# Multiplying the modulation tiles of a hybrid diffusion layer in runs of two and of four

## The chip, the core and the metric

The kernel runs on one core of a Trainium2 chip. The metric is the device time of one execution in microseconds, as the median of three runs. TensorE is called PE below, VectorE DVE, ScalarE ACT, GpSimd POOL and SyncE SP.

## What is computed

One layer of a diffusion trunk is applied, with the same weights, to 128 context tokens and 128 latent tokens. Cut to what matters here:

```python
mod  = silu(cond) @ w_mod + b_mod      # cond: (2048,), w_mod: (2048, 12288); one cond per token set
sh1, sc1, g1, sh2, sc2, g2 = split(mod, 6)
xm   = rmsnorm(x) * (1 + sc1) + sh1
u, q, k, v, g_s, g_a = split(xm @ w_in)
S    = glu(s5_scan(u))                 # 64 groups, 64 complex states, both directions
A    = windowed_attention(q, k, v)
x   += g1 * ((sigmoid(g_s) * (S @ w_ssm_o) + sigmoid(g_a) * (A @ w_attn_o)) @ w_out)
xm2  = rmsnorm(x) * (1 + sc2) + sh2
x   += g2 * (silu(a) * b @ w_down)     # a, b = split(conv3(xm2 @ w_up)), w_up: (2048, 11264)
```

Everything is float32. The big products are made of three matmuls each: a weight tile is split into a high and a low part (`hi`, `lo`), and so are the activations.

## The kernel before

**Weight tiles.** All weights come from DRAM in tiles of 128 x 1024 floats (512 KB), which SP's queue loads into five buffers (`raw`, `RAW = 5`). A tile of a big product is split by ACT (`hi`, L185) and DVE (`lo`, L186) into one of three pairs of buffers (`HL = 3`), and its raw buffer is free after the split. PE then multiplies it: a tile of `w_up` or `w_in` takes 24 matmuls on the full 128 x 128 array (L396 to L398).

**Modulation tiles.** `mod` has only two columns of activations, one for each token set. A tile of `w_mod` holds four K slices of 256 columns, and `mod_steps` multiplies it straight from its raw buffer, without a split, with four matmuls at L264. They use the array in tiles of 128 x 32, one K slice in each of the four groups of 32 columns. A raw buffer with a modulation tile becomes free when its matmuls are done. The float32 matmuls of L264 stand in the trace as two records each, so eight records are one tile.

**Stages and order.** Steps stand in one list, and `drive()` issues loads and splits ahead of them. First come the modulation tiles and the projections that the scan needs. In the scan stage the steps of the scan are woven with the rest of `w_in`, with `w_attn_o`, and with 96 modulation tiles (gate 1, shift 2, scale 2), each of which is a step of its own. Then come the GLU, the output projections, `w_out`, the second norm, and the up projection. The last 32 modulation tiles (`g2s`, gate 2) belong to the up projection: eight of them (`G2A`, `G2B`) wait in other buffers for the end of `w_out`; the others follow in the same raw buffers as `w_up`, `G2C` of them after every second step of `prep` (the second norm's transposes, L869, and the making of `xm2`), and the rest woven into the first 80% of the first third of the up projection.

The code is recorded in this order, and a scheduler then sets each engine's final order, so the engines' orders differ from the list.

Of the kernel before, what the change touches and what calls it, by code (L numbers as in the profile page):

```python
# [86 lines left out]
RAW, HL, W4, NS4, W2, LOADS = 5, 3, 18, 5, 3, 5  # L87
# [3 lines left out]
NGA2, NGS, SF0, ATT1 = 3, 4, 0.6, 1.0  # L91
ATTP, ATTH, OLS = 1, 300, False
FF0, FF1, MF0, MF1 = 0.0, 1.0, 0.0, 1.0
G2A, G2B, G2S, G2C, LAG2, HP2 = 8, 8, 3, 2, 2, 1000
FIRST_BANKS = ("acc", "acc", "acc", "y")


# [1 line left out]
def tile_hybrid_step(ctx, tc, a):  # L99
# [29 lines left out]
    def PS(shape, tag, bufs=1):  # L129
        return ps.tile(shape, F32, tag=tag, name=tag, bufs=bufs)  # L130

    def f32(x):
        return x.bitcast(F32)
# [6 lines left out]
    def drive():  # L140
        ch = [s for s in steps if s.src is not None]
        raws, hls = {}, {}
        cnt = {"raw": 0, "w4": 0, "first": 0, "s4": 0}
        cap = {"raw": RAW, "w4": LOADS, "first": 8, "s4": G2S}
        state = dict(nr=0, nh=0)

        def issue():
            c = ch[state["nr"]]
            if c.pre is not None:
                c.pre()  # L150
            if c.pool == "raw":
                r = rawp.tile([128, 2, 512], F32, tag="raw", name="raw")
            else:
                r = (T4 if c.pool == "first" else S4)([128, 2, 512], "rw4")
            for o, i in c.src(r):
                nc.sync.dma_start(o, i)
            raws[state["nr"]] = r
            cnt[c.pool] += 1
            state["nr"] += 1

        def ahead():
            while state["nr"] < len(ch) and cnt[ch[state["nr"]].pool] < cap[ch[state["nr"]].pool]:
                issue()

        ahead()
        idx = 0
        for st in steps:
            if st.src is None:
                st.fn()
                continue  # L170
            while state["nh"] < len(ch) and state["nh"] <= idx + HL - 1:
                n = state["nh"]
                while state["nr"] <= n:
                    issue()
                if ch[n].split:
                    if ch[n].hl:
                        th, tl = (ch[n].hl(x).rearrange("p (a b) c -> p a (b c)", a=2) for x in ("hi", "lo"))
                    else:
                        th = hlp.tile([128, 2, 512], F32R, tag="hi", name="hi")
                        tl = hlp.tile([128, 2, 512], F32R, tag="lo", name="lo")  # L180
                    w = slice(0, ch[n].nk)
                    with tc.high_priority(HP), ExitStack() as es:
                        for i in ch[n].after() if ch[n].after else ():
                            es.enter_context(tc.issue_after(i.ins))
                        ACT(th[:, w], raws[n][:, w], AF.Copy)  # L185
                        TT(tl[:, w], raws[n][:, w], f32(th[:, w]), OP.subtract)  # L186
                    hls[n] = (th, tl)
                    cnt[ch[n].pool] -= 1
                state["nh"] += 1
            ahead()  # L190
            if st.split:
                st.fn(*hls.pop(idx))
            else:
                st.fn(raws[idx])
                cnt[st.pool] -= st.frees
            raws.pop(idx)
            idx += 1
# [64 lines left out]
    def mod_mm(acc, kt, rhs, b, start, stop):  # L262
        j = kt % 4
        return MM(acc[32 * j:32 * j + 32], cst[:, kt, 6 - 2 * b:38 - 2 * b], rhs, start=start, stop=stop, skip_group_check=True,  # L264
           tile_position=(0, 32 * j))

    def mod_pp(acc, nb, blocks):
        m = T2([128, 512], "macc")[:, 0:acc.shape[1]]
        nc.vector.transpose(out=m, in_=acc)
        p = acc[:, 0:acc.shape[1] // 64 * nb].rearrange("p (c b s) -> p c b s", b=nb, s=2)  # L270
        mv = m.rearrange("p (c b r) -> p b c r", b=4, r=32)
        for b in range(4):
            MM(p[32 * b:32 * b + 32], i32r, mv[:, b, :, 0:2 * nb], start=True, stop=True, skip_group_check=True, tile_position=(0, 32 * b))
        for b0, c0, nc_, b, n in blocks:
            ks = slice(b0, b0 + nc_ * n)
            v = lambda t: t[:, ks].rearrange("p (b c) -> p c b", b=n)
            TT(modp[:, ks, :].rearrange("p (b c) s -> p c b s", b=n), p[:, c0:c0 + nc_, b:b + n, :],
               v(bT).unsqueeze(3).to_broadcast([128, nc_, n, 2]), OP.add)
# [15 lines left out]
        for s in range(2):  # L294
            nc.sync.dma_start(out[:, s, :], d[s:s + 1, 512 * cg:512 * cg + 512].to_broadcast([128, 512]))

    def mod_steps(gs, pool="raw"):
        nb = len(gs)
        st = {}

        def chunk(b, h, kq):
            def f(raw):
                if (b, h, kq) == (0, 0, 0):
                    st["a"] = PS([128, 512], "mod")
                r = raw.rearrange("p a c -> p (a c)").rearrange("p (k c) -> p k c", k=4)
                prev = None
                for j in range(4):
                    with tc.issue_after(prev.ins) if prev is not None else nullcontext():
                        prev = mod_mm(st["a"][:, 256 * h:256 * h + 256], 4 * kq + j, r[:, j, :], b, b == 0 and h == 0 and kq == 0, b + 1 == nb and kq == 3)
                if b + 1 == nb and (h, kq) == (1, 3):  # L310
                    one = all(g == gs[0] + i for i, g in enumerate(gs))
                    mod_pp(st["a"], nb, [(4 * gs[0], 0, 4, 0, nb)] if one else [(4 * g, 0, 4, i, 1) for i, g in enumerate(gs)])
            return f

        def src(g, h, kq):
            return lambda raw: [(raw, a["w_mod"][MOD_AT[g], h, kq])]
        return [Step(chunk(b, h, kq), src(g, h, kq), False, pool) for b, g in enumerate(gs) for h in range(2) for kq in range(4)]

    def mod_first(k0, n):
        v = a["w_mod_first"]  # L320
# [214 lines left out]
    def mod_phase(p):  # L535
        k0, n = sum(PHASES[:p]), PHASES[p]
        if n < 4:
            return mod_first(k0, n)
        return mod_steps([4 + k0 // 4, k0 // 4], "w4")
# [142 lines left out]
    def weave(main, *fills):  # L682
        n = len(main)
        pos = [0] * len(fills)
        for i, s_ in enumerate(main):
            steps.append(s_)
            for k, fl in enumerate(fills):
                fl, lo, hi = fl if isinstance(fl, tuple) else (fl, 0.0, 1.0)
                while pos[k] < len(fl) and pos[k] * (hi - lo) * n < (i + 1 - lo * n) * len(fl):
                    end = burst(fl, pos[k])  # L690
                    steps.extend(fl[pos[k]:end])
                    pos[k] = end
        for k, fl in enumerate(fills):
            steps.extend((fl[0] if isinstance(fl, tuple) else fl)[pos[k]:])
# [32 lines left out]
    fill += [u for i in range(NGS) for u in gs(i)]  # L727
    modfill = []
    for i in range(8, 20, 4):
        modfill += mod_steps(list(range(i, i + 4)))  # L730
    weave(ssm.stages(), (fill, FF0, FF1), (modfill, MF0, MF1))
    for i in range(NGS, 4):
        steps.extend(gs(i))
# [243 lines left out]
            gfb.append(t)  # L977

    CUT = [0, 8, 15, 22]
    g2s = mod_steps([20, 21, 22, 23])  # L980
    for x in g2s[:G2B]:
        x.pool = "first"

# [18 lines left out]
    g2s = g2s[G2A:]  # L1002
    for p in range(3):
# [3 lines left out]
        if p == 0:  # L1007
# [10 lines left out]
            for k in range(8):  # L1018
                step(lambda k=k: prep(k))
                if k >= LAG2:  # L1020
                    steps.append(ups[k - LAG2])
                    if k % 2 == 0:
                        steps.extend(g2s[:G2C])
                        g2s = g2s[G2C:]
# [11 lines left out]
    def final(s):  # L1036
        row_norm(s, 1)
        for h in range(2):
            t = x1t[2 * s + h]
            row_scale(t, t, s)  # L1040
            nc.sync.dma_start(yout[s][:, 1024 * h:1024 * h + 1024], t)

    drive()


# [459 lines left out]
```

## Time and profile before

| | |
|---|---|
| Time, median of 3 runs | 1558.11 us (1556.1 to 1558.49) |
| Time of the profiled execution | 1556.7 us |
| Its span, first to last instruction | 1554.9 us |
| PE busy | 1507.4 us (97%) |
| DVE, ACT busy | 1005.6 us, 767.1 us |
| Chain that ended last | PE 83%, DMA 6%, DVE 5%, ACT 3% |
| Loads from DRAM | 343.76 MB, 223 GB/s over the span |

The span is what the views of the trace show; the profiled execution's own time is 1.8 us longer. PE is named in most of the chain, so what PE does and what it waits for sets the time; the other engines count where PE waits for them. Overlapping matmuls are counted once in the busy time.

The stages in the trace, in us from its start: modulation and first projections to 260, scan stage 260 to 603, GLU and output projections to 761, second norm and up projection (first third) 761 to 945, the rest of the feed-forward part to 1555.

### The profile page before, as it was taken

The numbers are of one execution on the slowest core, as the hardware profiler recorded it, in microseconds if no ns is written. First come the engines' busy times: TensorE is split into PE (matmuls) and PEld (weight loads), VectorE is DVE, ScalarE is ACT, GpSimd is POOL, SyncE is SP. The second block draws the span as 40 slices with busy tenths as digits, with TensorE's granted clock in tenths as the row PEclk, the third lists the DMA queues.
The fourth block names the chain that finished last, engine by engine and source line by source line (L and its number), as shares of the span: only waits on it lengthen the run. The fifth ranks groups of instructions, "written<-read, shape, count | busy, mean of one in ns | idle before, by whom it ended". The sixth has DMA issues, their size and how long they took to land.

```text
span 1554.9 us, 30702 instructions
## 1 busy us (share of the span) xinstructions
PE 1507.4 (97%) x12575; PEld 1330.7 (86%) x12575; DVE 1005.6 (65%) x1541; ACT 767.1 (49%) x1191; POOL 85.7 (6%) x179
## 2 busy tenths in 40 slices
PE   6999999999899999999899999999999999999997
PEld 5768799788688888988699899889999988999986
DVE  4998687468776666665655556655656655666665
ACT  6334548545555567444544445433544533545543
POOL 2000014022322000000000000000000000000000
PEclk9999999999899999999999999999999999999999
DMA  9999754774577777866556665765555565565563
GB/s 348 362 367 306 267 192 167 249 284 146 181 266 248 264 264 272 312 218 200 190 186 237 222 226 189 246 200 189 170 197 180 177 202 190 176 203 195 172 204 121
DMA packets 104252, 349.28 MB, mean 225 GB/s; under 512 B 13900, under 2 KB 16628, under 8 KB 104112
## 3 DMA queue, kind: packets, MB, share of 16 engines
q1 hardware_dynamic: 98576, 344.20, 64.2%
q0 software_dynamic: 5312, 3.05, 0.9%
q8 instruction: 99, 1.62, 0.4%
q14 instruction: 41, 0.34, 0.1%
q10 hardware_dynamic: 224, 0.08, 0.0%
HBM read 343.76 MB, written 2.46 MB: 223 GB/s over the span
## 4 chain that ended last, share of the span: by engine, by line
PE 83%; DMA 6%; DVE 5%; ACT 3%; issue 1%; POOL 1%; SPq 0%; DVEq 0%; ACTq 0%
PE acc L396 16%; PE acc L397 15%; PE acc L398 15%; PE acc L422 8%; PE acc L423 8%; PE acc L424 8%; PE mod L264 5%; DMA raw<-in_w_in_dram 3%; DMA raw<-in_w_mod_dram 2%; DVE lo L186 2%; PE bu L1376 1%; ACT hi L185 1%; DMA U<-u 1%; ACT CL L1330 1%; POOL U L1317 1%
## 5 line engine op out<-in xcount | busy, mean ns | idle before, releaser
L186 DVE TENSOR_TENSOR lo<-raw,hi 128x1024 fp32r<-128x1024 f32 (+1 forms) x456 | 538.2, 1185 | 448.6 <-ACT hi L185 445.3
L185 ACT ACTIVATE hi<-raw 128x1024 fp32r<-128x1024 f32 (+1 forms) x456 | 468.1, 1028 | 597.2 <-PE acc L398 274.8
L396 PE MATMUL acc<-yh,lo 128*128 128x256 f32 x1408 | 401.3, 285 | 0.5 <-DVE lo L186 0.5
L397 PE MATMUL acc<-yl,hi 128*128 128x256 f32 x1408 | 399.5, 284 | 0.0
L398 PE MATMUL acc<-yh,hi 128*128 128x256 f32 x1408 | 399.3, 284 | 0.0
L396 PEld LDWEIGHTS acc<-yh,lo 128*128 128x128 f32 x1408 | 270.4, 192 | 9.0 <-DVE lo L186 3.0
L397 PEld LDWEIGHTS acc<-yl,hi 128*128 128x128 f32 x1408 | 270.9, 192 | 0.9 <-DVE m L875 0.8
L398 PEld LDWEIGHTS acc<-yh,hi 128*128 128x128 f32 x1408 | 270.8, 192 | 0.0
L396 PE MATMUL acc<-xh,lo 128*128 128x256 f32 x568 | 168.1, 296 | 4.7 <-ACT sig L673 2.6
L398 PE MATMUL acc<-xh,hi 128*128 128x256 f32 x568 | 161.7, 285 | 0.0
L397 PE MATMUL acc<-xl,hi 128*128 128x256 f32 x568 | 161.5, 284 | 0.0
L423 PE MATMUL acc<-lo,ff 128*128 128x512 f32 x352 | 136.9, 389 | 0.0
L424 PE MATMUL acc<-hi,ff 128*128 128x512 f32 x352 | 136.8, 389 | 0.0
L422 PE MATMUL acc<-hi,ff 128*128 128x512 f32 x352 | 127.8, 390 | 0.0
L396 PEld LDWEIGHTS acc<-xh,lo 128*128 128x128 f32 x568 | 108.2, 190 | 22.4 <-issue 8.4
L397 PEld LDWEIGHTS acc<-xl,hi 128*128 128x128 f32 x568 | 108.4, 191 | 1.4 <-issue 0.9
L398 PEld LDWEIGHTS acc<-xh,hi 128*128 128x128 f32 x568 | 108.2, 191 | 0.3 <-issue 0.2
L264 PE MATMUL mod<-raw,cst 128*32 128x256 f32 x960 | 82.6, 404 | 5.6 <-DMA raw<-in_w_mod_dram 4.8
L422 PEld LDWEIGHTS acc<-hi,ff 128*128 128x128 f32 x352 | 66.1, 188 | 14.6 <-issue 1.1
L424 PEld LDWEIGHTS acc<-hi,ff 128*128 128x128 f32 x352 | 66.1, 188 | 13.8
L423 PEld LDWEIGHTS acc<-lo,ff 128*128 128x128 f32 x352 | 66.1, 188 | 13.6
L1317 POOL DMA_DIRECT2D U<-u x128 | 62.6, 497 | 161.7 <-PE bu L1376 138.6
(365 smaller groups left out, 2172.7 us busy)
## 6 DMA issues: line engine op xcount, KB each, us to landing
raw<-in_w_up_dram SPq DMA_DIRECT2D x176, 512.0 KB, 4.2
raw<-in_w_mod_dram SPq DMA_DIRECT2D x120, 512.0 KB, 4.6
raw<-in_w_in_dram SPq DMA_DIRECT2D x88, 512.0 KB, 5.0
raw<-in_w_down_dram SPq DMA_DIRECT2D x88, 512.0 KB, 4.0
rw<-in_w_mod_dram SPq DMA_DIRECT2D x56, 512.0 KB, 5.8
raw<-in_w_out_dram SPq DMA_DIRECT2D x32, 512.0 KB, 4.3
rw<-in_w_mod_first_dram SPq DMA_DIRECT2D x16, 512.0 KB, 7.2
raw<-in_w_in_dram SPq DMA_DIRECT2D x32, 256.0 KB, 5.8
```

The source lines that it names most:

```text
L185: ACT(th[:, w], raws[n][:, w], AF.Copy)
L186: TT(tl[:, w], raws[n][:, w], f32(th[:, w]), OP.subtract)
L264: return MM(acc[32 * j:32 * j + 32], cst[:, kt, 6 - 2 * b:38 - 2 * b], rhs, start=start, stop=stop, skip_group_check=True, tile_position=( ...
L396: MM(o, wl, xh, start=start, stop=False, skip_group_check=True)
L397: MM(o, wh, xl, start=False, stop=False, skip_group_check=True)
L398: MM(o, wh, xh, start=False, stop=stop, skip_group_check=True)
L422: MM(accs[s], xl, hi[:, j, :], start=(kt == first), stop=False)
L423: MM(accs[s], xh, lo[:, j, :], start=False, stop=False)
L424: lastmm[0] = MM(accs[s], xh, hi[:, j, :], start=False, stop=(kt == last - 1))
L1317: nc.gpsimd.dma_start(G["U4", qd][32 * e:32 * e + 32, q, :], u[32 * q:32 * q + 32, 64 * e:64 * e + 64])
L1330: ACT(CL[ri][hs, 1:4, :, h, :], tC[hs, ri], AF.Copy, scale=-1.0 if ri else 1.0)
L1376: MM(bu[:, ri, x], BL[d][:, ri, q, :], u[:, :, ::-1] if d else u, start=(x == 0), stop=True, skip_group_check=True)
```

## The change

Modulation tiles are multiplied in runs. `mod_steps` gets a number `run`: the matmuls of `run` successive tiles are issued together when the last of them is there, the last landed tile first. In the scan stage `run` is 2, in the up projection 4. A tile's step then frees no buffer until the run's last step frees all of them (`frees`), and `drive()` gets a rule that it looks no further ahead for splits while a run is incomplete and the five raw buffers are taken. `G2C` goes from 2 to 4, so that the up projection's runs stay whole.

```diff
-G2A, G2B, G2S, G2C, LAG2, HP2 = 8, 8, 3, 2, 2, 1000
+G2A, G2B, G2S, G2C, LAG2, HP2 = 8, 8, 3, 4, 2, 1000
...
                 n = state["nh"]
+                if state["nr"] <= n and cnt["raw"] >= RAW and not st.frees:
+                    break
                 while state["nr"] <= n:
...
-    def mod_steps(gs, pool="raw"):
+    def mod_steps(gs, pool="raw", run=1):
         nb = len(gs)
-        st = {}
+        st = {"r": []}
...
-                r = raw.rearrange("p a c -> p (a c)").rearrange("p (k c) -> p k c", k=4)
+                st["r"].append((kq, raw.rearrange("p a c -> p (a c)").rearrange("p (k c) -> p k c", k=4)))
+                if len(st["r"]) < run:
+                    return
                 prev = None
-                for j in range(4):
-                    with tc.issue_after(prev.ins) if prev is not None else nullcontext():
-                        prev = mod_mm(st["a"][:, 256 * h:256 * h + 256], 4 * kq + j, r[:, j, :], b, b == 0 and h == 0 and kq == 0, b + 1 == nb and kq == 3)
+                q0 = st["r"][0][0]
+                for q, r in st["r"][::-1]:
+                    for j in range(4):
+                        with tc.issue_after(prev.ins) if prev is not None else nullcontext():
+                            prev = mod_mm(st["a"][:, 256 * h:256 * h + 256], 4 * q + j, r[:, j, :], b,
+                                          b == 0 and h == 0 and q0 == 0 and q == kq, b + 1 == nb and kq == 3 and q == q0)
+                st["r"].clear()
...
-        return [Step(chunk(b, h, kq), src(g, h, kq), False, pool) for b, g in enumerate(gs) for h in range(2) for kq in range(4)]
+        return [Step(chunk(b, h, kq), src(g, h, kq), False, pool, frees=0 if (kq + 1) % run else run)
+                for b, g in enumerate(gs) for h in range(2) for kq in range(4)]
...
-        modfill += mod_steps(list(range(i, i + 4)))
+        modfill += mod_steps(list(range(i, i + 4)), run=2)
...
-    g2s = mod_steps([20, 21, 22, 23])
+    g2s = mod_steps([20, 21, 22, 23], run=4)
```

No instruction is added or removed: PE has 10845 matmuls in both, 832 of them at L264 (L266 in the change, whose lines are 2 to 9 further down). The scheduler orders all engines anew. Counted over PE's whole order, two neighbouring matmuls use different tilings of the array (128 x 128 against 128 x 32) 328 times before and 266 times in the change, 160 against 135 of these in the scan stage and 54 against 18 in the up projection. The 96 modulation tiles of the scan stage stand in 70 pieces before and in 57 in the change, the 32 of the up projection in 25 and in 7.

PE's order where the second norm ends and the up projection begins, before (`mod` are modulation tiles, `n2` and L869 the norm's transposes, `acc` the first `w_up` tile):

```order
L264 MATMUL mod_9022<-raw_8911,cst_105 32x256 x4
L264 MATMUL mod_9022<-raw_8929,cst_105 32x256 x4
L869 MATMUL misc_9063<-kc_90,n2_9019 128x128 x4
L869 MATMUL y_9077<-kc_90,n2_9019 128x128 x4
L264 MATMUL mod_9022<-raw_9051,cst_105 32x256 x4
L869 MATMUL misc_9094<-kc_90,n2_9089 128x128 x4
L396 MATMUL acc_9106<-yh_9061,lo_9048 128x256
L264 MATMUL mod_9022<-raw_9136,cst_105 32x256 x4
L869 MATMUL misc_9197<-kc_90,n2_9192 128x128 x4
L869 MATMUL y_9154<-kc_90,n2_9089 128x128 x4
L264 MATMUL mod_9022<-raw_9166,cst_105 32x256 x4
L397 MATMUL acc_9106<-yl_9062,hi_9047 128x256
```

And in the change:

```order
L266 MATMUL mod_9022<-raw_8965,cst_105 32x256 x4
L266 MATMUL mod_9022<-raw_8947,cst_105 32x256 x4
L266 MATMUL mod_9022<-raw_8929,cst_105 32x256 x4
L266 MATMUL mod_9022<-raw_8911,cst_105 32x256 x4
L878 MATMUL misc_9063<-kc_90,n2_9019 128x128 x4
L878 MATMUL y_9077<-kc_90,n2_9019 128x128 x4
L878 MATMUL misc_9094<-kc_90,n2_9089 128x128 x4
L405 MATMUL acc_9106<-yh_9061,lo_9040 128x256
L878 MATMUL y_9160<-kc_90,n2_9089 128x128 x4
L878 MATMUL misc_9209<-kc_90,n2_9204 128x128 x4
L406 MATMUL acc_9106<-yl_9062,hi_9039 128x256
```

Four modulation tiles stand ahead of the transposes instead of two, and the three that stood between the transposes and the first `w_up` tile are gone from there.

SP's queue at the same place, right after the last `w_out` tile; before:

```order
L156 DMA raw_8893<-in_w_up_dram 128x1024
L156 DMA raw_8911<-in_w_mod_dram 128x1024
L156 DMA raw_8929<-in_w_mod_dram 128x1024
L156 DMA raw_8947<-in_w_up_dram 128x1024
L156 DMA raw_8965<-in_w_up_dram 128x1024
L156 DMA raw_9051<-in_w_mod_dram 128x1024
```

And in the change:

```order
L156 DMA raw_8893<-in_w_up_dram 128x1024
L156 DMA raw_8911<-in_w_mod_dram 128x1024
L156 DMA raw_8929<-in_w_mod_dram 128x1024
L156 DMA raw_8947<-in_w_mod_dram 128x1024
L156 DMA raw_8965<-in_w_mod_dram 128x1024
L156 DMA raw_9043<-in_w_up_dram 128x1024
L156 DMA raw_9136<-in_w_up_dram 128x1024
L156 DMA raw_9142<-in_w_mod_dram 128x1024
```

The second and third `w_up` tile are loaded after the first four modulation tiles instead of with them: five loads fill the five buffers, so these two wait until PE has multiplied modulation tiles.

SP's queue at one of the two late runs of the up projection, in the change (the fifteen loads before and after are of `w_up`):

```order
L156 DMA raw_9724<-in_w_up_dram 128x1024
L156 DMA raw_9754<-in_w_mod_dram 128x1024
L156 DMA raw_9802<-in_w_mod_dram 128x1024
L156 DMA raw_9834<-in_w_mod_dram 128x1024
L156 DMA raw_9864<-in_w_mod_dram 128x1024
L156 DMA raw_9894<-in_w_up_dram 128x1024
L156 DMA raw_9972<-in_w_up_dram 128x1024
L156 DMA raw_9978<-in_w_up_dram 128x1024
```

And at about that place before:

```order
L156 DMA raw_9792<-in_w_up_dram 128x1024
L156 DMA raw_9798<-in_w_mod_dram 128x1024
L156 DMA raw_9828<-in_w_up_dram 128x1024
L156 DMA raw_9858<-in_w_up_dram 128x1024
L156 DMA raw_9868<-in_w_up_dram 128x1024
L156 DMA raw_9870<-in_w_mod_dram 128x1024
L156 DMA raw_9924<-in_w_up_dram 128x1024
```

One modulation tile stood between two or three `w_up` tiles; now four stand together and hold four of the five buffers until they are multiplied. By the built program's addresses, `raw_9894` and after it `raw_9972` share the fifth buffer, and `raw_9978` takes one that the run has freed.

## Rows read from the trace of the kernel before

**Rows 1.** The page: span, and rate of the loads in 40 slices.

```profile
span 1554.9 us, 30702 instructions
GB/s 348 362 367 306 267 192 167 249 284 146 181 266 248 264 264 272 312 218 200 190 186 237 222 226 189 246 200 189 170 197 180 177 202 190 176 203 195 172 204 121
```

**Rows 2.** PE around one modulation tile, in order of time.

```profile
865.91 0.28 PE L398 MATMUL acc<-yh,hi 128*128 128x256 f32 x1
866.12 0.64 PE L264 MATMUL mod<-raw,cst 128*32 128x256 f32 x8
866.69 0.39 PE L396 MATMUL acc<-yh,lo 128*128 128x256 f32 x1
866.91 0.28 PE L397 MATMUL acc<-yl,hi 128*128 128x256 f32 x1
867.03 0.28 PE L398 MATMUL acc<-yh,hi 128*128 128x256 f32 x1
```

**Rows 3.** PE around two modulation tiles that stand together, in order of time.

```profile
506.12 0.28 PE L398 MATMUL acc<-xh,hi 128*128 128x256 f32 x1
506.33 1.07 PE L264 MATMUL mod<-raw,cst 128*32 128x256 f32 x16
507.33 0.39 PE L396 MATMUL acc<-xh,lo 128*128 128x256 f32 x1
507.55 0.28 PE L397 MATMUL acc<-xl,hi 128*128 128x256 f32 x1
```

**Rows 4.** PE from the last modulation tiles to the first `w_up` tile, in order.

```profile
764.42 1.05 PE L264 MATMUL mod<-raw,cst 128*32 128x256 f32 x16
...
768.43 0.64 PE L264 MATMUL mod<-raw,cst 128*32 128x256 f32 x8 [1.72 <-DMA raw<-in_w_mod_dram]
...
773.58 1.12 PE L869 MATMUL y<-kc,n 128*128 128x128 f32 x4 [1.21 <-DVE m L875]
776.08 1.08 PE L264 MATMUL mod<-raw,cst 128*32 128x256 f32 x8 [1.38 <-DMA raw<-in_w_mod_dram]
777.08 0.58 PE L397 MATMUL acc<-yl,hi 128*128 128x256 f32 x1
```

**Rows 5.** ACT in the same stretch, in order of time.

```profile
763.80 2.94 ACT L185 ACTIVATE hi<-raw 128x1024 fp32r<-128x1024 f32 x3
766.65 1.48 ACT L877 ACTIVATE m<-misc,modp,gsc 128x128 f32<-128x128 f32 x4
768.16 0.63 ACT L879 ACTIVATE yh<-m 128x512 fp32r<-128x512 f32 x1
```

**Rows 6.** DVE in the same stretch, in order of time.

```profile
769.91 2.34 DVE L186 TENSOR_TENSOR lo<-raw,hi 128x1024 fp32r<-128x1024 f32 x2
772.18 1.35 DVE L875 TENSOR_SCALAR m<-y,gsc,modp 128x128 f32<-128x128 f32 x4
773.46 1.87 DVE L880 TENSOR_TENSOR yl<-m,yh 128x512 fp32r<-128x512 f32 x3
```

**Rows 7.** Busy time and granted clock (PEclk) by stretches of the span.

```profile
770.00:777.08 7.08, 4.09 (x24) 1.64 (x16) 6.67 (x14) 4.69 (x12) 0.00 (x0) 0.50 0.87 282
777.08:781.00 3.92, 3.92 (x25) 3.92 (x22) 1.24 (x2) 0.43 (x1) 0.00 (x0) 0.60 0.52 187
...
370.00:400.00 30.00, 22.08 (x330) 18.96 (x333) 22.70 (x45) 21.39 (x57) 7.82 (x16) 0.91 0.15 52
400.00:603.00 203.00, 197.59 (x2579) 165.50 (x2571) 134.51 (x212) 114.59 (x229) 23.47 (x48) 0.98 0.72 255
```

**Rows 8.** The chain that ended last, one tile's load and split in the scan stage.

```profile
472.07 3.21 DMA raw<-in_w_in_dram
...
475.37 1.07 ACT hi L185
...
476.46 1.24 DVE lo L186
```

**Rows 9.** DMA issues by line: KB each, median us from issue to landing.

```profile
raw<-in_w_up_dram SPq DMA_DIRECT2D x176, 512.0 KB, 4.2
```

## The prediction

> **What bounds the kernel.** I read the page first, then the busy time by stretches, then PE in order of time, and last the loads. PE sets the time: in the main stretch of the scan stage it is busy 197.6 of 203 us, and from 370 to 400 us, where it is idle for 7.9 of 30 us, it is the scan's own chain over ACT and DVE that it waits for [rows 7]. The whole span is 1554.9 us [rows 1]; the profiled execution took 1556.7, 1.8 more, and the median of the runs is 1558.1, another 1.4 more. So I sum against 1556.7 and add 1.4.
>
> In PE's own time the thing to see is what a modulation tile costs in a stream of other matmuls. Such matmuls start 0.12 us apart (866.91 and 867.03). From the last one before a tile (865.91) to the second one after it (866.91) it is 1.00 us instead of 0.24, so the tile costs 0.76 [rows 2]. Two tiles together take 506.12 to 507.55, 1.43 instead of 0.24, so 1.19 [rows 3]. The second tile thus costs 0.43, and 0.33 of a tile that stands alone is entering and leaving: the first tile record starts 0.21 after the matmul before it, and the two matmuls behind it are 0.22 apart. Each visit less is worth 0.33 us on PE if nothing else changes.
>
> The second place is the gap between `w_out` and the up projection. The stream of `w_up` matmuls begins at 777.08, and before it PE waits twice for a modulation tile (1.72 and 1.38 us) and once for DVE (1.21) [rows 4]. The granted clock there is 0.50, the lower of its two levels (1.2 and 2.4 GHz), and still 0.60 up to 781 [rows 7].
>
> **What the change does, part by part.** The work is the same; only order and buffers change.
>
> *Visits.* There are 62 changes of tiling less on PE, so 31 visits: 12.5 in the scan stage, 18 in the up projection, one half each way elsewhere. At 0.33 that would be 10.2 us.
>
> *Scan stage.* By position in the built order, 6.5 of the 12.5 visits go away before about 405 us, and 6 after it. The early ones shorten work ahead of the stretch where PE waits for ACT and DVE anyhow [rows 7], so I count them at nothing (at most 2.1 us). The late ones count, 6 x 0.33 = 2.0. Against them stands that the first tile of a pair keeps its buffer until the second has landed. A load of 0.524 MB at the best rate of a slice, 362 GB/s, takes 1.45 us [rows 1], and the weight tile behind it comes up to that much later. One tile through one buffer takes 3.21 + 1.07 + 1.24 = 5.5 us, 5.6 with the queue [rows 8]. Counted in PE's work between the freeing of a buffer and the use of the tile in it, the tightest weight tile of the scan stage has 5.9 us before and 5.1 in the change, and the tenth part with the least has up to 7.1 before and 6.0 in the change. So few loads come late, and by tenths. I take 0; the bounds are 0 and one transfer for every eighth of 48 pairs, 6 x 1.45 = 8.7. Scan stage: -2.0, between -4.1 and +6.7.
>
> *The gap.* Now four tiles stand ahead of the transposes. They begin at 764.42, and two more tiles at 0.43 put the transposes at 766.3 instead of 765.4 [rows 3, 4]. ACT was busy with three splits until 766.65 [rows 5]; two of those now wait for their loads, so it takes the first transposes at about 767.0, 1.5 us of them, then the split of the second `w_up` tile (1.07), 0.63 for `yh`, the third tile's split (1.07), and the second transposes' 1.5: 772.8. DVE, which split two tiles first (2.34 us) [rows 6], does `m` (1.35) at 769.9, one split (1.24) and `yl` (0.6): 773.1. The last transposes follow at 772.8 and take up to 1.1 us at the lower clock [rows 4], so the stream begins near 773.8 instead of 777.08, 3.3 us earlier. One tile less lies behind it (12 against 13), 0.43. Gain 2.9; nothing if the loads of the two `w_up` tiles, issued at 765.1, land late (6 us instead of the row's 3.21 would do it).
>
> *The up projection's visits.* After 777 us, 21 visits become 6: 15 x 0.33 = 5.0. An idle 0.4 us at 808 goes too.
>
> *The run of four and the buffers.* This is the wait that the change adds. Four modulation tiles hold four of five buffers until the last has landed and all are multiplied. The fifth passes one `w_up` tile after another: the next tile cannot be loaded before DVE has split the one in the buffer, 5.6 us per tile [rows 8], and PE uses a tile in 24 x 0.12 = 2.9 us [rows 2]. SP's queue is in order, so the loads behind wait as well. What covers this is three split tiles in stock, and the run itself, 0.33 + 4 x 0.43 = 2.05 us. The skill's rule speaks against it: the Trainium skill, page "Trainium Kernel Development and Optimization", section Best Practices, asks to double-buffer so that transfers overlap with compute, and a run of four leaves a single buffer; by that rule the run would cost more than its visits give back, as in the second rival below.
>
> For a late run, take S as the start of the third last tile ahead of the run. The last of the three is split by S + 2.4, the fifth buffer's new tile is in it and split 5.6 + 0.7 later (DVE also has the group's end), S + 8.7, and the tile after that at S + 14.3. PE is through three tiles at S + 8.6, through the run at S + 10.7, through the first tile at S + 13.55: it waits 0.75. With the median landing of 4.2 instead of 3.21 [rows 9] twice, 2.75. Two late runs: 1.5, between 0 and 5.5.
>
> The early runs follow each other with two tiles between. Third run: the load of the tile behind it stands behind four loads of modulation tiles that start at 783.3, so it lands after five transfers, 792.5, and is split at 794.9; PE is through the run at 793.6 and waits 1.3. Fourth run: its last tile lands 0.7 late, and the tile behind it 1.6. The sum is 3.6; the lower clock at the start, which delays PE and not the loads, hides about 1.1. I take 2.5, between 0 and 6.
>
> Up projection: -2.9 - 5.0 - 0.4 + 2.5 + 1.5 = -4.3, between -8.3 and +6.1.
>
> *The rest.* One visit less around the GLU, -0.3. The two lines in `drive()` add no instruction.
>
> **Sum.** -2.0 - 4.3 - 0.3 = -6.6: 1550.1 for a profiled execution, 1551.5 for the median.
>
> **Rivals.**
>
> 1. *The waits eat the gain* (no change, 0.17). For it: SP's queue is in order, and the medians of landing are above 3.21. The late runs at 2.75 and the early ones at 6 cost 11.5, against 10.6 of gains (5.0 + 0.4 + 2.9 + 2.0 + 0.3): 1559. Against it: stocks of three split tiles, and at the early runs the gap's 3 us.
>
> 2. *The single buffer starves PE* (slower, 0.09). Place: the first two `w_up` tiles behind each of the six runs. Each comes 5.6 - 2.9 = 2.7 late, together 5.4, and only the run's 2.05 covers it: 6 x 3.35 = 20 us, 1558.1 - 10.6 + 20 = 1567.5. It decides from 10.6 / 6 = 1.8 us of waiting per run. The scan's 8.7 us for the pairs would come to the same side. Against it: before the run there are split tiles in stock, so the first of the two is in time.
>
> 3. *Everything comes in* (faster by more, 0.15): no wait at the runs, all of the scan's visits. 1558.1 - 10.6 - 2.1 = 1545.4.
>
> 4. *The change doesn't do what it says.* The scheduler could split the runs again. It does so in a few places (48 pairs stand in 57 pieces), and these are in the count already.
>
> **The numbers.** The likeliest, the sum above, has 0.59, with a range of its own of 1548 to 1555. A measurement of this kernel can tell about 0.2%, 3.1 us, from no change: faster means below 1555.0, slower above 1561.2. Faster: 0.59 and 0.15, of which I take off a little for the upper end of the first, 0.73. Same 0.18, slower 0.09. The range leaves out the ends of rivals 2 and 3 and half of rival 1: 1546 to 1558.5.
>
> **What the profile after would show.** Modulation records in runs of 32 in the up projection and 16 in most of the scan stage, a run of 32 costing 2.05 us in the stream. The stream of `w_up` begins 3 us earlier after the last `w_out` matmul. PE waits on `lo` L188 behind the third to sixth run, 0.5 to 2 us each. Scan stage shorter by 2 us, the time from the last `w_out` matmul to the end of the first third by 4. Wrong: if the stream begins no earlier, if a run waits more than 2 us, or if PE waits for weight tiles in the scan stage at many pairs.

## The result and the profile after

The change takes 1568.78 us (median of 4 runs, 1567.45 to 1573.05), the kernel before 1557.11 beside it: a ratio of 1.0072, with a 95% interval of 1.0053 to 1.0092. I had forecast 1551.5, faster. It is slower by 11.7 us. The profiled execution of the change is the slowest of its four, 1573.05 us with a span of 1570.9, so its trace shows 16.0 us more than the one before, of which some 4 are its own. 2.3 of the 16.0 arise in the first 30 us, where no run of the change stands: a group of 32 modulation records takes 1.94 us there instead of 1.08 (at 21.33 us; before at 20.69), and from then on all of the first stage is 2.3 later. e13 below, which has single tiles, shows 1.94 there too, so this comes about without runs.

The page of the change, with its span, the groups of PE that waited most (busy, mean ns of one, then the idle time before them and what ended it), and the median landing of `w_up` loads:

```profile
span 1570.9 us, 30700 instructions
...
L405 PE MATMUL acc<-yh,lo 128*128 128x256 f32 x1408 | 401.2, 285 | 8.7 <-DVE lo L188 7.1
...
L405 PE MATMUL acc<-xh,lo 128*128 128x256 f32 x568 | 168.4, 297 | 11.9 <-ACT sig L682 6.3
...
L266 PE MATMUL mod<-raw,cst 128*32 128x256 f32 x960 | 72.1, 397 | 7.8 <-DMA raw<-in_w_mod_dram 7.7
...
raw<-in_w_up_dram SPq DMA_DIRECT2D x176, 512.0 KB, 4.0
```

The same groups on the page of the kernel before, and its median landing for `w_in`, which [rows 9] left out:

```profile
L396 PE MATMUL acc<-yh,lo 128*128 128x256 f32 x1408 | 401.3, 285 | 0.5 <-DVE lo L186 0.5
...
L396 PE MATMUL acc<-xh,lo 128*128 128x256 f32 x568 | 168.1, 296 | 4.7 <-ACT sig L673 2.6
...
L264 PE MATMUL mod<-raw,cst 128*32 128x256 f32 x960 | 82.6, 404 | 5.6 <-DMA raw<-in_w_mod_dram 4.8
...
raw<-in_w_in_dram SPq DMA_DIRECT2D x88, 512.0 KB, 5.0
```

The saved visits are there: the modulation matmuls are busy 72.1 us instead of 82.6. But PE stands idle 28.4 us ahead of these three groups instead of 10.8. A single load is not slower in general: the median landing is 4.0 us for `w_up` against 4.2 [rows 9] and 4.4 for `w_in` against 5.0, but 5.0 for modulation tiles against 4.6.

Where it happens is read by stages. I cut each trace where five matmuls into `acc` start on PE, counted from the beginning (the 960th, 2352nd, 3288th, 3312th and 4824th; 24 are one split tile). They bound the first stage, the scan stage, GLU and output projections, the gap up to the end of the first `w_up` tile, and the first eight groups of the up projection. (Before, those end at 980 us; the 945 that stands with the table of before is about where the last modulation tile was done.) GLU and output projections take 151.9 to 153.7 us in all kernels below, what follows the eight groups, up to the last of these matmuls, 563.9 or 564.0. The four that differ, in us of one profiled execution each:

| kernel | median | first | scan | gap | up |
|---|---|---|---|---|---|
| before | 1557.1 | 258.6 | 347.0 | 21.3 | 201.3 |
| the change | 1568.8 | 260.9 | 359.4 | 17.8 | 206.5 |
| e1 pairs alone, last first | 1571.4 | 261.0 | 356.8 | 20.6 | 201.9 |
| e2 fours alone, last first | 1560.1 | 258.6 | 347.7 | 17.7 | 206.7 |
| e3 the change, landed order | 1555.2 | 259.0 | 351.3 | 19.1 | 198.8 |
| e5 landed order, last touched first | 1572.4 | 261.1 | 356.8 | 16.9 | 206.8 |
| e8 fours alone, landed order | 1554.1 | 258.6 | 348.8 | 18.1 | 197.1 |
| e15 pairs alone, landed order | 1561.3 | 258.9 | 349.4 | 23.6 | 201.5 |
| e12 single tiles, 4 buffers | 1577.4 | 270.4 | 358.5 | 17.6 | 200.9 |
| e13 single tiles, 5, NS4 = 4 | 1565.2 | 265.0 | 345.4 | 21.2 | 201.5 |
| e6 single tiles, 6, NS4 = 4 | 1557.6 | 268.5 | 341.9 | 19.8 | 199.4 |
| e14 the change, 5, NS4 = 4 | 1569.9 | 265.5 | 350.7 | 18.0 | 207.2 |
| e4 the change, 6, NS4 = 4 | 1550.0 | 267.8 | 335.6 | 21.6 | 195.2 |
| e7 landed order, 6, NS4 = 4 | 1550.9 | 269.8 | 341.7 | 17.6 | 194.6 |

In the change the scan stage has grown by 12.4 us and the up projection by 5.2, and the gap has shrunk by 3.5.

**The scan stage.** PE's busy time in it (first figure behind the length), before and in the change:

```profile
258.60:605.60 347.00, 331.32 (x4006) 276.72 (x4005) 233.50 (x382) 201.62 (x411) 50.19 (x102) 0.98 0.67 237
```

```profile
260.90:620.30 359.40, 330.61 (x4014) 281.89 (x4013) 234.58 (x385) 201.19 (x411) 52.28 (x106) 0.97 0.65 230
```

The idle time is 28.8 us instead of 15.7, and the busy time is nearly the same. Two changes cancel in it. The saved visits are there: the stage's 768 modulation records are busy 59.9 us instead of 64.2. But PE runs longer at the lower of its two levels (1.2 instead of 2.4 GHz). Over this stage, read in stretches of 20 us, the granted clock falls short of 1.00 by 12.0 us in all (20 times the shortfall of each stretch), before by 7.0. The two lowest stretches of the change (the granted clock is the third figure from the end):

```profile
400.00:420.00 20.00, 14.41 (x145) 10.00 (x146) 12.93 (x26) 12.94 (x32) 1.64 (x4) 0.77 0.58 207
...
520.00:540.00 20.00, 14.88 (x147) 11.71 (x147) 6.34 (x13) 14.67 (x32) 0.00 (x0) 0.83 0.64 226
```

So a wait also costs what the clock takes after it, about 5 us here, which is more than the stage's visits save. The largest parts of the idle time by what ended them (total, times, longest), before:

```profile
PE y L1339 <- ACT u L1429: 3.2, 2, 2.9
PE acc L396 <- ACT sig L673: 2.6, 2, 2.0
PE mod L264 <- DMA raw<-in_w_mod_dram: 1.7, 3, 0.9
...
PE acc L396 <- DVE lo L186: 1.1, 3, 0.5
```

and in the change:

```profile
PE mod L266 <- DMA raw<-in_w_mod_dram: 7.0, 4, 3.8
PE acc L405 <- DVE lo L188: 6.3, 5, 1.7
PE acc L405 <- ACT sig L682: 6.3, 2, 4.0
```

These three went from 5.4 to 19.6 us. The first two are loads that come late. The third is an evacuation that ACT does, and ACT itself waited longer for loads: its splits of `w_in` tiles stood 69.3 us for them in this stage instead of 52.2 (ACT's own waits). The longest wait for it, and ACT ahead of it:

```profile
525.12 0.58 PE L405 MATMUL acc<-xh,lo 128*128 128x256 f32 x1 [4.00 <-ACT sig L682]
```

```profile
512.16 1.06 ACT L187 ACTIVATE hi<-raw 128x1024 fp32r<-128x1024 f32 x1 [4.83 <-DMA raw<-in_w_in_dram]
...
515.59 1.06 ACT L187 ACTIVATE hi<-raw 128x1024 fp32r<-128x1024 f32 x1 [1.22 <-DMA raw<-in_w_in_dram]
...
524.47 0.60 ACT L682 ACTIVATE sig<-acc 128x512 f32<-128x512 f32 x1
```

Between the second split and `sig` ACT isn't idle: the scan's work, which stood behind the splits, and two loads of ACT's tables of 1.28 us each fill that time.

**The gap.** PE in the change, from the last `w_out` matmul (774.97) on; it answers to [rows 4]:

```profile
774.97 0.39 PE L433 MATMUL acc<-hi,mh 128*128 128x512 f32 x1
775.29 3.66 PE L266 MATMUL mod<-rw,cst 128*32 128x256 f32 x64
778.76 1.91 PE L266 MATMUL mod<-raw,cst 128*32 128x256 f32 x32
780.60 0.66 PE L878 MATMUL misc<-kc,n 128*128 128x128 f32 x4
...
784.86 0.51 PE L405 MATMUL acc<-yh,lo 128*128 128x256 f32 x2 [1.35 <-ACT yh L888]
...
787.97 0.56 PE L406 MATMUL acc<-yl,hi 128*128 128x256 f32 x1
```

The stream begins 13.0 us after the last `w_out` matmul. Before it was 777.08 [rows 4] less 760.62, where that matmul starts there, 16.5. The transposes now wait for ACT (1.16 and 0.87 us) and DVE (0.29), not for the loads of modulation tiles.

**The up projection.** PE around the first late run, the fifth of the six (32 records, four tiles):

```profile
867.05 0.28 PE L407 MATMUL acc<-yh,hi 128*128 128x256 f32 x1
867.26 1.94 PE L266 MATMUL mod<-raw,cst 128*32 128x256 f32 x32
869.13 0.39 PE L405 MATMUL acc<-yh,lo 128*128 128x256 f32 x1
869.35 0.28 PE L406 MATMUL acc<-yl,hi 128*128 128x256 f32 x1
...
874.10 0.39 PE L405 MATMUL acc<-yh,lo 128*128 128x256 f32 x1 [1.83 <-DVE lo L188]
```

The run costs 869.35 - 867.05 - 0.24 = 2.06 us. One `w_up` tile behind it was split in time; the second makes PE wait 1.83. SP's queue shows why, and ACT behind it:

```profile
868.24 7.39 SPq L156 DMA_DIRECT2D raw<-in_w_up_dram  x7
```

```profile
865.89 1.06 ACT L187 ACTIVATE hi<-raw 128x1024 fp32r<-128x1024 f32 x1 [6.10 <-DMA raw<-in_w_up_dram]
871.73 1.06 ACT L187 ACTIVATE hi<-raw 128x1024 fp32r<-128x1024 f32 x1 [4.78 <-DMA raw<-in_w_up_dram]
```

After a pause since 861.08 seven loads are issued within 7.4 us. The one at 868.24 takes the fifth buffer, out of which DVE had split a tile until 868.22, the others those that the run frees; ACT stands for the first of them until 871.73. The wait has a second price here too. The granted clock right behind it:

```profile
874.00:875.00 1.00, 0.90 (x7) 0.90 (x8) 0.99 (x2) 0.02 (x1) 0.00 (x0) 0.96 1.02 401
875.00:876.00 1.00, 1.00 (x7) 1.00 (x7) 0.27 (x1) 0.49 (x1) 0.00 (x0) 0.50 0.99 406
...
878.00:879.00 1.00, 1.00 (x9) 1.00 (x9) 0.70 (x2) 0.23 (x1) 0.00 (x0) 0.83 0.91 340
```

PE runs at the lower of its two levels for three of these microseconds; over 870 to 880 the mean is 0.83, a loss of 1.7 us. All waits of PE in the stage:

```profile
PE acc L405 <- DVE lo L188: 7.1, 6, 1.8
PE mod L266 <- DMA raw<-in_w_mod_dram: 0.7, 1, 0.7
```

### The profile page after: what moved, and what is told of

The parts are those of the page before. It is cut to its first block, busy times and chain, and to the rows that moved or that the text cites. A ratio compares the mean times of both kernels' runs of the same rounds, so it can differ in the third digit from the quotient of the medians.

```text
span 1570.9 us, 30700 instructions
## 1 busy us (share of the span) xinstructions
PE 1503.9 (96%) x12575; PEld 1339.7 (85%) x12575; DVE 1004.8 (64%) x1541; ACT 765.2 (49%) x1191; POOL 85.7 (5%) x179
## 4 chain that ended last, share of the span: by engine, by line
PE 81%; DMA 8%; ACT 5%; DVE 4%; issue 1%; POOL 1%; SPq 0%; ACTq 0%; DVEq 0%
PE acc L405 15%; PE acc L406 15%; PE acc L407 15%; PE acc L431 8%; PE acc L432 8%; PE acc L433 8%; PE mod L266 5%; DMA raw<-in_w_in_dram 3%; DMA raw<-in_w_mod_dram 2%; DVE lo L188 2%; DMA raw<-in_w_up_dram 2%; ACT hi L187 2%; PE bu L1385 1%; PE misc L1318 1%; ACT CL L1339 1%
## 5 line engine op out<-in xcount | busy, mean ns | idle before, releaser
L266 PE MATMUL mod<-raw,cst 128*32 128x256 f32 x960 | 72.1, 397 | 7.8 <-DMA raw<-in_w_mod_dram 7.7
```

## The experiments

Theory A, later H: a run holds its buffers until its last tile has landed and all are multiplied, and with five buffers the loads behind it come late. Rivals: only the fours cost (B), PE's wait for the last tile or the reversed order costs (C, F, W), or the scheduler's new order of the other work does (D). Ratios are to the kernel before on the same chip, with 95% intervals. The experiments ran on three chips (e1 to e4 and e9 to e12 on one, e5 to e8 on a second, e13 to e15 on a third), so where two of different chips are compared the ratios tell more than the medians.

**e1 and e2: each part alone.**

```diff
-    g2s = mod_steps([20, 21, 22, 23], run=4)        # e1, and G2C = 2
+    g2s = mod_steps([20, 21, 22, 23])
-        modfill += mod_steps(list(range(i, i + 4)), run=2)     # e2
+        modfill += mod_steps(list(range(i, i + 4)))
```

> Only the scan stage's modulation tiles are multiplied in pairs; the up projection has single tiles and G2C = 2 as before. In the trace of the change the scan stage (from the 260 us mark to the end of the 608th weight tile's worth of matmuls) is about 11 us longer than before and the up projection about 6 longer, the gap between them 3 shorter; that profiled execution was itself 4 us above the median of the change. Theory A (a pair holds two of five buffers until its second tile has landed and both are multiplied, so the loads behind start late and together): most of the loss is here, about +7 to +9 us, 1564 to 1566. Theory B (the loss is the up projection's, by its runs of four, and the scan stage's part of it is chance): 1555 to 1558. If the scan stage's gain of my prediction held, 1555.

> Only the up projection's modulation tiles are multiplied in runs of four (G2C = 4); the scan stage has single tiles. Theory A: the gap is 3 us shorter, the waits for lo behind the runs cost 8 and the visits give 5 back, with a lower clock behind the gap: about +2.5 us, 1559 to 1560. Theory B: +8 to +11, 1565 to 1568. If e1 and e2 add up to the change's 11.7, the two parts don't work on each other.

e1 took 1571.4 us, 1.0077 (1.0056 to 1.0097); e2 1560.1, 1.0008 (0.9993 to 1.0023). The pairs alone cost all that the change costs, and more than theory A said; the fours alone make no difference that can be told. Theory B fell. Together the two ratios come to 0.85%, the change's is 0.72%, so within the intervals the parts don't work on each other. In e2 the gap gives 3.6 us and the up projection loses 5.4.

**e3: the tiles of a run in the order in which they landed.**

```diff
-                for q, r in st["r"][::-1]:
+                for q, r in st["r"]:
...
```

The line that marks the first and the last matmul of an accumulation follows the order; it is left out here and in e5.

> The change, with each run multiplied in the order in which its tiles landed instead of the last landed first. The oldest tile's buffer, which the queue's next load takes, is then free 0.43 us earlier in a pair and 1.3 us earlier in a run of four, and PE can begin a run while its last tile is still on the way. Theory A: the waits shrink by about that, 2 to 5 us in all, 1564 to 1567. Theory C (the reversed order is the whole loss: PE stands idle ahead of a run for the last tile while the others are there): 1557 or less. Theory D (the order of the buffers doesn't matter, the scheduler's new order of the other work does): 1568 to 1569.

1555.2 us, 0.9967 (0.9953 to 0.9981): 13.6 less than the change, 1.05% by the ratios, and faster than before. Theory A's 1564 to 1567 missed, and the time is in theory C's range. So the reversed order carries the whole loss. It does so by more than the order, as the trace shows: in landed order a tile can go when it has landed. Counted in the traces, the tiles of the scan stage stand in 65 pieces against the change's 64, but in 10 of 48 pairs the first is done before the second has landed (in none of the change). The up projection's tiles stand in 13 pieces instead of 7, as in e8 below, whose PE rows show that only some are whole runs:

```profile
793.06 1.93 PE L266 MATMUL mod<-raw,cst 128*32 128x256 f32 x32
798.37 0.64 PE L266 MATMUL mod<-raw,cst 128*32 128x256 f32 x8
800.19 0.64 PE L266 MATMUL mod<-raw,cst 128*32 128x256 f32 x8 [1.18 <-DMA raw<-in_w_mod_dram]
803.82 1.07 PE L266 MATMUL mod<-raw,cst 128*32 128x256 f32 x16
```

**e4: the change with six raw buffers.**

```diff
-RAW, HL, W4, NS4, W2, LOADS = 5, 3, 18, 5, 3, 5
+RAW, HL, W4, NS4, W2, LOADS = 6, 3, 18, 4, 3, 5
```

> The change with six raw buffers instead of five; the space comes from NS4 = 4 instead of 5 (one buffer less for the norm's and the gates' tiles). Theory A: the waits behind the runs shrink to what they were before, and most of the 11.7 us comes back: 1554 to 1560. Theory D (the order of the other work): 1566 to 1570. That NS4 = 4 costs something by itself is possible; the kernel before with the same two numbers will be the control.

1550.0 us, 0.9946 (0.9926 to 0.9966), with the runs and the reversed order as in the change: more than theory A said comes back. PE's waits in the scan stage, those for `lo` and `sig`; one for a modulation tile's load is no longer among them:

```profile
PE acc L405 <- ACT sig L682: 1.5, 2, 0.8
...
PE acc L405 <- DVE lo L188: 0.7, 1, 0.7
```

**e5: what of the order costs.** The landed order, but one matmul of the last tile first.

```diff
-                for q, r in st["r"][::-1]:
-                    for j in range(4):
+                seq = [(kq, 0, st["r"][-1][1])] + [(q, j, r) for q, r in st["r"] for j in range(4) if (q, j) != (kq, 0)]
+                for q, j, r in seq:
...
```

> The change, with each run in the order in which its tiles landed, but with one matmul of the last tile put ahead of them. So PE begins a run only when its last tile has landed, as in the change (1568.8 and 1571.4 with pairs reversed, e1), while the oldest buffer is free after five of a pair's eight matmuls, nearly as early as in e3 (1555.2). SP's queue is the same in all of them. Theory F (the order in which the buffers come free costs the time, since the queue's next load takes the oldest one): 1555 to 1558. Theory W (the wait for the last tile ahead of the run costs it, and with it what the scheduler can put between): 1566 to 1570.

1572.4 us, 1.0093 (1.0076 to 1.0110). Theory F fell: freeing the oldest buffer first doesn't bring the time back. What costs is that the run waits for its last tile, with all that goes with it. But PE hardly stands idle for that tile in e5; its longest waits in the scan stage are these, with 0.9 us for modulation tiles' loads:

```profile
PE acc L405 <- DVE lo L188: 7.4, 5, 2.7
PE acc L405 <- ACT sig L682: 5.7, 2, 3.1
PE y L1348 <- ACT u L1438: 4.5, 2, 2.8
```

So theory C's idle time ahead of the run isn't needed for the loss; here it stands behind the run, at the weight tiles and at ACT. In the change both occur: of its 13.1 us of new idle time 5.3 end with a modulation tile's load.

How long buffers are held I took from the traces, for the 96 modulation tiles of the scan stage: from the issue of a tile's load to the start of the last of its eight records, plus 0.2 us, with loads and tiles matched in order. The mean for the two tiles of a pair together is 24.9 us before, 26.6 in the change, 26.1 in e1, 26.3 in e5, but 24.9 in e3 and 24.7 in e15. The three that wait for the last tile hold a pair's buffers 1.2 to 1.7 us longer, and these three lose the 10 to 12 us in the scan stage. (In e14 and e13 below it is 25.3 against 25.0, and 5.3 us are lost, so the loss doesn't follow the holding time alone.)

**e6 and e7: six buffers with single tiles, and in landed order.** e6 is the kernel before and e7 is e3, with e4's line of sizes.

> The kernel before with single tiles, with six raw buffers and NS4 = 4, the control of e4 (1550.0). If five buffers are too few for the kernel before as well, this gains as e4 does: 1548 to 1553, and pairs and fours are worth nothing even with room. If runs are worth their saved visits once the buffers suffice (about 10 us by the count of visits), this stays at 1556 to 1560. If NS4 = 4 costs something, it is above 1559.

> e4 (six raw buffers, the change's runs) with the tiles of a run in the order in which they landed. If the sixth buffer covers what the reversed order costs, it equals e4: 1548 to 1551. If the reversed order still costs something with six, 1545 to 1547.

e6: 1557.6, 0.9994 (0.9983 to 1.0005). e7: 1550.9, 0.9935 (0.9916 to 0.9954), the same as e4. With room, runs beat single tiles by 0.5 to 0.6%, some 7 to 9 us (e4 and e7 against e6), and their order makes no difference that can be told.

**e8: fours alone in landed order** (e2 with e3's line).

> Single tiles in the scan stage, and runs of four in the up projection in the order in which they landed (G2C = 4), with five buffers. e2, the same with the last landed first, gave 1560.1 (no change); in the profile of e3 the gap and the up projection up to the end of its first third are 4.7 us shorter than before, and the scan stage 4.3 longer. Theory A or F (buffers): the scan stage is as before and the up projection keeps e3's gain: 1553 to 1556. If fours don't gain in this order either: 1558 to 1561.

1554.1, 0.9966 (0.9954 to 0.9979), as theory A said: the gap keeps its 3.2 us and the up projection is 4.2 shorter.

**e9 to e11: the sixth buffer only from the scan stage on**, in e4, e7 and e6.

```diff
+    capr = [RAW - 1]
-... cnt[ch[state["nr"]].pool] < cap[ch[state["nr"]].pool]:
+... cnt[ch[state["nr"]].pool] < (capr[0] if ch[state["nr"]].pool == "raw" else cap[ch[state["nr"]].pool]):
     step(ssm.setup)
+    step(lambda: capr.__setitem__(0, RAW))
```

> e4 (six buffers, runs with the last landed first), but the loads may fill the sixth buffer only from the start of the scan stage on. In e6 (six buffers, single tiles) the matmuls up to the 260 us mark come 9.9 us later than before, nearly all of it between 82 and 137 us, where the queue's order has a weight tile more ahead of the first modulation tiles. If that order is the reason, this loses the 9.1 us of e4's profile at that mark: 1540 to 1543. If NS4 = 4 is the reason, it stays at 1549 to 1551. Theory H (a run's buffers are held until its last tile has landed, and five are too few for that): the reversed order is as good as the landed order here.

> e7 (six buffers, runs in the order in which they landed), with the sixth buffer only from the scan stage on. As e9: 1540 to 1543 if the queue's order in the first stage cost the 10 us, 1549 to 1552 if NS4 = 4 did. Theory H: equal to e9 within 2 us. If the reversed order costs PE time of its own even with room, this is 5 us or more below e9.

> e6 (six buffers, single tiles), with the sixth buffer only from the scan stage on: the control of e9 and e10. In e6's profile the stage behind the 260 us mark is 5 us shorter than before in the scan and 3 in the rest. If the first stage's loss goes, 1548 to 1551, and the runs are then worth 7 to 8 us with six buffers, about the 10 that the count of visits gave; if this comes to 1543 as well, the sixth buffer gives the gain and the runs nothing.

1548.5, 0.9942 (0.9922 to 0.9962); 1549.8, 0.9942 (0.9923 to 0.9961); 1556.5, 0.9991 (0.9977 to 1.0005). My guess on the first stage was wrong: its marks stay at 265.2 to 267.1 us, so the sixth buffer's loads ahead were not what delays it. (In e9 and e10 the new rule of `drive()` goes by `capr` too.) On theory H all three agree with e4, e7 and e6.

**e12: single tiles with four buffers** (RAW = 4 in the kernel before).

> The kernel before (single tiles) with four raw buffers instead of five: what one buffer less costs by itself. In the change the buffer of a pair's first tile is held 1.8 us longer from the issue of its load to the end of its matmuls (14.7 against 12.9, mean of 48), which takes some 48 x 1.8 = 86 us of buffer time out of five buffers over a scan stage of 350 us, a quarter of one buffer. Theory H: this kernel loses clearly more than the change did, 1580 to 1620. If the number of buffers hardly matters to single tiles (as the sixth didn't: 1557.6), 1559 to 1565, and theory H would be in doubt.

1577.4, 1.0128 (1.0109 to 1.0148), a little under theory H's range. Its scan stage has 358.5 us, as much as the change's 359.4: pairs with the last landed first cost there what a whole buffer less costs.

**e13 and e14: NS4 = 4 with five buffers**, single tiles and the change's runs (`5, 3, 18, 4, 3, 5`).

> The kernel before with NS4 = 4 and its five raw buffers. If NS4 = 4 is what delays the first stage in e6 and e11 (by 6.6 to 9.9 us at the 260 us mark), this is 1565 to 1569, and the sixth buffer then gave single tiles 8 to 10 us (1557.6 and 1556.5). If NS4 = 4 costs nothing, 1557 to 1561, and the delay of the first stage belongs to the sixth buffer.

> The change (last landed first) with NS4 = 4 and five raw buffers. Theory H (five buffers are too few for the runs, the sixth brought e4 and e9 down): as slow as the change or slower by NS4's cost, 1568 to 1580, about 20 to 30 us above e4 and e9 (1550.0 and 1548.5). If NS4 = 4 was what helped: 1549 to 1556.

e13: 1565.2, 1.0024 (1.0012 to 1.0036). e14: 1569.9, 1.0056 (1.0035 to 1.0076). NS4 = 4 is most of what delays the first stage (its mark is at 265.0 and 265.5, 258.6 before). Against these two the sixth buffer gives single tiles 0.3% by the ratios (e6, e11), some 5 us, and the change's runs 1.1% (e4, e9), some 17. The medians differ by 8 and 20 us, but they are from different chips.

**e15: pairs alone in landed order** (e1 with e3's line).

> e1 (pairs in the scan stage alone, single tiles in the up projection, G2C = 2) in the order in which the tiles landed. e3 (1555.2) and e8 (1554.1) differ by the scan's pairs, so with five buffers these should be worth nothing: 1558 to 1561, 10 to 12 us below e1 (1571.4). If the pairs' saved visits come in: 1553 to 1556. If they cost time by themselves, whatever the order: 1565 and more.

1561.3, 1.0014 (0.9997 to 1.0030): no difference from single tiles. With five buffers the pairs' saved visits come to nothing even so.

## Why the prediction was wrong

**The step that failed** is the scan stage's "So few loads come late, and by tenths. I take 0", in the sum -2.0. It came out as +9.8 (e1's profile) to +12.4, beyond my upper bound of +6.7 too. Three things were wrong in it. I set the slack of each weight tile against 5.6 us, made from one load of 3.21 [rows 8], a quick one. The page's median for `w_in` is 5.0, and 5.0 + 1.07 + 1.24 is 7.3, more than the slack of my tenth part (7.1 before, 6.0 in the change). By this count five buffers were already at their edge, which the page would have told. And I priced a late load by one transfer of 1.45 us on PE. In the trace it also stands ahead of the scan's work and of `sig` in ACT's order, and 3.7 of the 13.1 us of new idle time come through `sig` alone. And I gave the waits no price in clock: the stage falls short of full clock by some 5 us more than before. The best slice's rate is 367 GB/s, not 362 [rows 1], which changes the 1.45 us by 0.02. The 2.3 us of the first 30 us stand in no term of the sum.

**Right: the cost of a visit.** A run of 32 records costs 2.06 us (2.05 forecast), and the up projection's modulation tiles stand in 7 pieces. In the scan stage the modulation records are busy 4.3 us less, near the 4.1 of 12.5 visits at 0.33. With six buffers, where PE waits only 0.7 us for `lo` in e4's scan stage, the runs gain 7 to 9 us over single tiles.

**Right: the gap.** Forecast 3.3 us earlier for the start of the stream, measured 16.5 - 13.0 = 3.5.

**Too small: the waits behind the fours.** I took 4.0 us (2.5 and 1.5), between 0 and 11.5; the trace has 7.1 + 0.7 = 7.8. The mechanism is the one described, seen at 868 to 874. I left out the clock: its mean is 0.83 over 870 to 880 us, 1.7 us, and 0.85 over 790 to 800, 1.5 us; the first microsecond of this stretch lost about 0.5 before as well [rows 7], so 2.7 are new. Thus -5.0 - 0.4 + 7.8 + 2.7 = +5.1 against +5.2 measured.

**The rivals.** The time is near the second rival's 1567.5, but not by its place: the fours, for which it was worked out, cost nothing on balance (e2), and I had only mentioned the pairs there. The Trainium skill's rule that I set against the change (page "Trainium Kernel Development and Optimization", section Best Practices, to overlap transfers with compute by double-buffering) pointed the right way, and the trace agrees: 5.3 of the 13.1 us of new idle time in the scan stage end with a modulation tile's load, 5.2 with a weight tile's split. With a sixth buffer the same runs are some 17 us faster (e14, e4), single tiles some 5 (e13, e6).

**What stays open.** Whether it is the longer holding of a pair's buffers, or where the scheduler puts other work when a run can't start before its last tile, was not told apart: both go with the wait for the last tile, and the loss vanishes with the sixth buffer. The space of the sixth buffer was taken from NS4 in every run, so what six buffers would give with NS4 = 5, without the first stage's loss, wasn't tried.

## What to carry to other kernels

Batching work that reads straight from load buffers saves switches on the engine, but a run that waits for its last tile also holds its buffers longer, and here the loads and splits behind it came late: work out the time of one buffer's round with the median landing of the page, not with one quick load, and see what is over. Let each tile go as it lands, unless there is a buffer to spare; here the order of a loop decided between 0.7% slower and 0.3% faster. A late load is paid for on each engine that handles it in order, so price it with all that stands behind it there, and with what the clock takes after PE's wait.

## What the runs showed of the hardware

A wait of 1.83 us on PE, in the middle of a stream that had run at full clock, was followed by three microseconds at half of it (0.50 from 875 to 878 us), so that it cost nearly twice its length; the wait of 1.46 us before 811.9 and that of 1.69 before 822.9 had no such effect (the clock stays at 1.00 from 810 to 830). In the scan stage of the same trace a wait of 1.68 us before 290.6 did have it (0.51 from 291.2 to 294.7 us), so in this trace the length of a wait alone doesn't tell what the clock does after it.
